# Encoder trunk on one core: the feed forward's activations turned by VectorE and memory in place of TensorE

## The chip, the core and the metric

The kernel runs on one core of a Trainium2 chip. The metric is device time in microseconds for one execution, median of three. TensorE (PE in the profile, PEld for its weight loads) multiplies, VectorE (DVE) and ScalarE (ACT) do the element work, SyncE (SP) issues the transfers between memory and the core, GpSimd (POOL) does little here.

## What is computed

Two layers over 256 tokens of 1024 features; the part that the change touches is the feed forward at the end of each layer:

```
def swiglu(hn, w_gu, w_down):
    g, u = jnp.split(hn @ w_gu, 2, axis=-1)
    return (jax.nn.silu(g) * u) @ w_down

for l in range(DEPTH):
    ...                                   # projections, three attentions, cross attention
    x = x + swiglu(rmsnorm(x, norm_ffn[l]), w_gu[l], w_down[l])
return rmsnorm(x, final_norm)
```

`w_gu` is 1024 x 5632, `w_down` is 2816 x 1024, all in float32.

## The kernel before

**Weights in chunks.** All weights lie in memory in the order of use, cut into 315 chunks of at most 128 x 1024 elements (512 KB). SP loads a chunk into one of 4 raw buffers (`wr`). ACT rounds it into `wh` (L192, fp32r) and DVE subtracts to get the rest, `wl` (L193); of these pairs there are 9. A product is three fast matmuls: `xh*wh`, `xh*wl`, `xl*wh` (L375, L376, L377). A chunk in the feed forward holds two blocks of 128 rows by 512 columns, so each half of the tokens needs six matmuls of it and both need twelve.

**Two halves.** The 256 tokens are two programs of 128 tokens, t = 0 and t = 1. They go through the chunks in the same order, t = 1 five calls behind (LAG); a chunk's buffer pair is free when t = 1 is through with it. `mm` yields before each chunk and calls `bg_step` after it; `defer(act)` puts an action off until the second such step after it.

**Feed forward.** For f = 0 to 4: four chunks of the gate weights give `ga`, then ACT takes the tanh (L795) and DVE multiplies (L796); four chunks of the up weights give `ua`, and DVE makes the activations `hh` (L805), 128 tokens x 512 features. f = 5 has 256 features and both parts in one product. The down projection needs `hh` with features on the partitions: `trans4` (L250) turns it by four TensorE transposes against the identity into PSUM (two for f = 5), and `split` rounds it into `hi` and `lo` (L241 on ACT, L242 on DVE). The six turned tiles of a half are the 22 blocks of features that the two products `fd0` and `fd1` then use.

**Order.** A scheduler sets the order of each engine's instructions at compile time, from priorities (program order, with `urgent` parts ahead) and its own estimate of when things are ready. Every engine, SP's queue of transfers included, works through its list in that order, and a waiting instruction holds up those behind it. `t2k` tiles (`t` in names) are 8 buffers that both halves share, `s2` tiles (`m`) are 11 for each half.

Of the kernel before, what the change touches and what calls it, by code (L numbers as in the profile page):

```python
# [12 lines left out]
F32 = mybir.dt.float32  # L13
F32R = mybir.dt.float32r
# [4 lines left out]
P = 128  # L19
# [18 lines left out]
LAG_OF = {(l, name): i + 1 for l in range(DEPTH) for i, name in enumerate(FIRST[l])}  # L38
WARM = 5
RAWBUFS = 4  # L40
AHEAD = 1
RAW_AHEAD = 4

# [68 lines left out]
def body(nc, tc, a, out, ctx):  # L112
# [4 lines left out]
    sb = ctx.enter_context(tc.tile_pool(name="sb", bufs=1))  # L117
    sm = ctx.enter_context(tc.tile_pool(name="sm", bufs=1))
    ps = ctx.enter_context(tc.tile_pool(name="ps", bufs=1, space=PS))
    V, S, T = nc.vector, nc.scalar, nc.tensor  # L120

    uid = [0]

    def nm(s):
        uid[0] += 1
        return f"{s}_{uid[0]}"

    def t2k(dtype=F32):
        return sb.tile([P, 512], dtype, name=nm("t"), tag="t2k", bufs=T2K)
# [4 lines left out]
    def psum(tag):  # L134
        return ps.tile([P, 512], F32, name=nm(tag), tag=tag, bufs={"acc": 3, "tp": 3, "sc": 2}[tag])
# [43 lines left out]
    def load_raw(c):  # L179
        g = c.group  # L180
        r = wp.tile([P, 1024], F32, name=nm("wr"), tag="wr", bufs=RAWBUFS)
        n = c.nkt * g.n
# [14 lines left out]
    def ensure(index):  # L197
        while split_next[0] <= min(index + AHEAD, len(chunks) - 1):
            i = split_next[0]
            while raw_next[0] <= min(i + RAW_AHEAD - 1, len(chunks) - 1):  # L200
                load_raw(chunks[raw_next[0]])
                raw_next[0] += 1
            split_chunk(i)
# [35 lines left out]
    def split(hi, lo, src, scale=None):  # L239
        if scale is None:  # L240
            S.activation(hi, src, AF.Copy)  # L241
            V.tensor_tensor(lo, src, hi.bitcast(F32), op=ALU.subtract)  # L242
        else:
            S.activation(hi, src, AF.Copy, scale=scale)
            V.scalar_tensor_tensor(lo, src, scale, hi.bitcast(F32), op0=ALU.mult, op1=ALU.subtract)

    def trans4(src, n=4, tag="tp"):
        tp = psum(tag)
        for i in range(n):
            T.transpose(tp[:, i * P:(i + 1) * P], src[:, i * P:(i + 1) * P], ident)  # L250
        return tp

    class Lhs:


# [7 lines left out]
    def split_tiles(t, tag, bufs):  # L263
        return (sb.tile([P, 512], F32R, name=nm("xh"), tag=f"{tag}{t}", bufs=bufs),
                sb.tile([P, 512], F32R, name=nm("xl"), tag=f"{tag}{t}", bufs=bufs))
# [50 lines left out]
    for p in range(4):  # L316
        hi, lo = split_tiles(p // 2, "x2_", X2BUFS)
# [17 lines left out]
    def program(t):  # L335
        bg = deque()

        later = deque()
# [8 lines left out]
                except StopIteration:  # L347
                    bg.popleft()

        def defer(act):  # L350

            later.append(lambda: later.append(act))

        def flush(gen):
            while later:
# [4 lines left out]
        def s2(dtype=F32):  # L360
            return sb.tile([P, 512], dtype, name=nm("m"), tag=f"m{t}", bufs=11)

        def mm(g, pairs):

            for c in g.chunks:
                yield
                ensure(c.index)
                hi, lo = splits[c.index]
                for lhs, acc in pairs:
                    for j in range(c.nkt):  # L370
                        kt = c.kt0 + j
                        xh, xl = lhs.blocks[kt]
                        wh, wl = hi[:, j * g.n:(j + 1) * g.n], lo[:, j * g.n:(j + 1) * g.n]
                        o = acc[:, :g.n]
                        T.matmul(o, xh, wh, start=kt == 0, stop=False)  # L375
                        T.matmul(o, xh, wl, start=False, stop=False)  # L376
                        T.matmul(o, xl, wh, start=False, stop=kt == g.kts - 1)  # L377
                bg_step()
# [51 lines left out]
        def pv_T(eTs, vs, pairs, nblk):  # L430

            in_line = line()
            o = psum("tp")
            with tc.high_priority(offset=150):
                for j, b in reversed(list(enumerate(pairs))):
                    for half in (1, 0):
                        c = (2 * b + half) * 64  # L440
                        for kb in reversed(range(nblk)):
                            in_line(T.matmul(o[half * 64:half * 64 + 64, j * P:(j + 1) * P], vs[kb][:, c:c + 64],  # L442
                                             eTs[half][j * nblk + kb], start=kb == nblk - 1, stop=kb == 0))
            return o
# [129 lines left out]
        for l in range(DEPTH):  # L574
# [34 lines left out]
            def indexer(acc):  # L609
                qi, ki = t2k(), t2k()  # L610
                rope(qi[:, :256], acc[:, :256], 4, rs8, t)
                rope(ki[:, :64], acc[:, 256:320], 1, rs, t)
                V.tensor_copy(ki[:, 64:128], ki[:, 0:64])
                V.tensor_scalar(wi[:, 0:4], acc[:, 320:324], rs[:, 0:1], 0.5, op0=ALU.mult, op1=ALU.mult)

                def turn_idx():
                    tp = psum("tp")
                    for i in range(2):
                        T.transpose(tp[:, i * P:(i + 1) * P], qi[:, i * P:(i + 1) * P], ident)
                    T.transpose(tp[:, 256:384], ki[:, 0:128], ident)  # L620
                    S.copy(qkiT, tp[:, 0:384])
                defer(turn_idx)

            branches = {}
            for br in "CBA":
# [3 lines left out]
                for name in FIRST[l] if br == "C" else [br + x for x in "qkv"]:  # L629
# [14 lines left out]
                    dst = s2()  # L644
                    if nme == "v":
                        S.activation(dst, acc, AF.Copy, scale=rs[:, 0:1])
                    else:
                        r_ = rs8 if nme == "q" else rs
                        tok = t2k()
                        if br == "A":  # L650
                            S.activation(tok, acc, AF.Copy, scale=r_[:, 0:1])
                        else:
                            rope(tok, acc, 8, r_, t)

                        def turn(tok=tok, dst=dst):
                            S.copy(dst, trans4(tok))
                        defer(turn)
# [7 lines left out]
                else:  # L665
                    gen = attn_A(l, ts_["q"])
                branches[br] = (gen, ts_["q"])
                defer(lambda gen=gen: bg.append(gen))

            y = None  # L670
# [24 lines left out]
            with urgent(t):  # L695
                for h in range(2):
                    tp = trans4(y[h])
                    hi, lo = split_tiles(t, "x2_", X2BUFS)
# [25 lines left out]
            if t == 0:  # L724
# [4 lines left out]
                for m in range(2):  # L729
                    tok = t2k()  # L730
                    S.activation(tok[:, :256], accs[m][:, :256], AF.Copy, scale=rsm[m])
                    tp = trans4(tok, 2)
# [6 lines left out]
            with urgent(t):  # L739
                qx, qxT = t2k(), t2k()  # L740
                S.activation(qx[:, :256], acc[:, :256], AF.Copy, scale=rs8[:, 0:1])
                tp = trans4(qx, 2)
# [28 lines left out]
            with urgent(t):  # L771
                eTs = [turn_over(e) for e in es]
                tp = pv_T(eTs, [vx[:, 0:256], vx[:, 256:512]], [0, 1], 2)
                hi, lo = split_tiles(t, "o2_", 2)
# [14 lines left out]
            for f in range(6):  # L789
                th, hh = t2k(), t2k()  # L790
                n = 512 if f < 5 else 256
                if f < 5:
                    ga = psum("acc")
                    yield from mm(G[f"fg{f}"], [(xf, ga)])
                    S.activation(th, ga, AF.Tanh, scale=rsh[:, 0:1])  # L795
                    V.scalar_tensor_tensor(th, th, 1.0, ga, op0=ALU.add, op1=ALU.mult)  # L796
                    ua = psum("acc")
                    yield from mm(G[f"fu{f}"], [(xf, ua)])
                else:
                    ga = psum("acc")  # L800
                    yield from mm(G["fgu"], [(xf, ga)])
                    S.activation(th[:, :n], ga[:, :n], AF.Tanh, scale=rsh[:, 0:1])
                    V.scalar_tensor_tensor(th[:, :n], th[:, :n], 1.0, ga[:, :n], op0=ALU.add, op1=ALU.mult)
                    ua = ga[:, n:2 * n]
                V.scalar_tensor_tensor(hh[:, :n], th[:, :n], rr2[:, 0:1], ua[:, :n], op0=ALU.mult, op1=ALU.mult)  # L805
                tp = trans4(hh, n // P)
                if f < 5:
                    hi, lo = s2(F32R), s2(F32R)
                else:
                    both = s2(F32R)  # L810
                    hi, lo = both[:, 0:256], both[:, 256:512]
                split(hi[:, :n], lo[:, :n], tp[:, :n])
                hT.add(hi, lo, n // P)
            ssq = small()
            xg = []
# [15 lines left out]
        for h, eng in enumerate((nc.scalar, nc.sync)):  # L831
            eng.dma_start(out[t * P:(t + 1) * P, h * 512:(h + 1) * 512], xg[h])

    progs = [program(0), program(1)]
    live = [True, True]

# [76 lines left out]
```

## Time and profile before

| | |
|---|---|
| median of 3 runs | 996.78 us (995.95 to 997.38) |
| profiled execution | 996.93 us, span 995.2 us |
| TensorE | busy 982.2 us (99%), granted clock 0.999 |
| VectorE, ScalarE | busy 661.1 us (66%), 561.2 us (56%) |
| transfers | 174.52 MB, mean 175 GB/s; SP's queue 55.4% of the 16 engines |
| feed forwards | first `hh` at 324.5 us, last at 937.6 us, in two stretches of some 115 us |

A row of the timeline gives the start, the time until the row's last instruction ends, engine, line and operation, the tiles written and read, the count, and in brackets the engine's idle time before and what ended it. Matmuls overlap: one that lasts 0.39 us is followed by the next after 0.23 us, so TensorE's pace is read from the starts.

### The profile page before, as it was taken

The numbers are of one execution on the slowest core, as the hardware profiler recorded it, in microseconds if no ns is written. First come the engines' busy times: TensorE is split into PE (matmuls) and PEld (weight loads), VectorE is DVE, ScalarE is ACT, GpSimd is POOL, SyncE is SP. The second block draws the span as 40 slices with busy tenths as digits, with TensorE's granted clock in tenths as the row PEclk, the third lists the DMA queues.
The fourth block names the chain that finished last, engine by engine and source line by source line (L and its number), as shares of the span: only waits on it lengthen the run. The fifth ranks groups of instructions, "written<-read, shape, count | busy, mean of one in ns | idle before, by whom it ended". The sixth has DMA issues, their size and how long they took to land.

```text
span 995.2 us, 13980 instructions
## 1 busy us (share of the span) xinstructions
PE 982.2 (99%) x5110; PEld 805.6 (81%) x5110; DVE 661.1 (66%) x1259; ACT 561.2 (56%) x985; POOL 14.0 (1%) x29
## 2 busy tenths in 40 slices
PE   8999999999999999999999999999999999999997
PEld 6887888888887888888888888888878778888885
DVE  5899666566866656554587995765676665656552
ACT  7546775555766544444554476764566764444441
POOL 0000000000000000000000000000000000000000
PEclk9999999999999999999999999999999999999999
DMA  8854445567662666666565545345566436656551
GB/s 301 281 185 149 142 133 150 151 189 236 207 188 71 205 177 188 188 178 191 174 209 200 168 131 166 128 150 168 190 214 191 147 106 191 190 175 208 188 169 43
DMA packets 50325, 174.52 MB, mean 175 GB/s; under 512 B 5712, under 2 KB 6608, under 8 KB 50000
## 3 DMA queue, kind: packets, MB, share of 16 engines
q1 hardware_dynamic: 49680, 172.94, 55.4%
q8 instruction: 40, 0.66, 0.3%
q10 hardware_dynamic: 576, 0.68, 0.2%
q14 instruction: 29, 0.24, 0.1%
HBM read 172.55 MB, written 1.05 MB: 174 GB/s over the span
## 4 chain that ended last, share of the span: by engine, by line
PE 90%; DVE 4%; DMA 2%; ACT 2%; issue 1%; SPq 0%; POOLq 0%; DVEq 0%; ACTq 0%
PE acc L375 27%; PE acc L376 27%; PE acc L377 26%; PE tp L250 4%; DVE wl L193 2%; PE tp L442 2%; PE sc L396 1%; DMA wr<-w_dram 1%; DMA t<-memT_dram 1%; PE sc L250 1%; PE tp L396 1%; ACT wh L192 1%; PE sc L748 1%; PE tp L426 1%; ACT m L276 0%
## 5 line engine op out<-in xcount | busy, mean ns | idle before, releaser
L193 DVE TENSOR_TENSOR wl<-wr,wh 128x1024 fp32r<-128x1024 f32 (+3 forms) x315 | 382.4, 1216 | 238.6 <-ACT wh L192 238.3
L192 ACT ACTIVATE wh<-wr 128x1024 fp32r<-128x1024 f32 (+3 forms) x315 | 331.6, 1054 | 262.2 <-PE acc L377 229.1
L375 PE MATMUL acc<-wh,xh 128*128 128x512 f32 (+2 forms) x1072 | 422.5, 395 | 1.7 <-ACT xh L276 0.9
L377 PE MATMUL acc<-wh,xl 128*128 128x512 f32 (+2 forms) x1072 | 416.3, 389 | 0.0
L376 PE MATMUL acc<-wl,xh 128*128 128x512 f32 (+2 forms) x1072 | 413.8, 387 | 2.0 <-DVE wl L193 2.0
L375 PEld LDWEIGHTS acc<-wh,xh 128*128 128x128 f32 x1072 | 202.0, 189 | 42.9 <-ACT xh L276 2.5
L376 PEld LDWEIGHTS acc<-wl,xh 128*128 128x128 f32 x1072 | 202.1, 189 | 41.6 <-DVE wl L193 4.2
L377 PEld LDWEIGHTS acc<-wh,xl 128*128 128x128 f32 x1072 | 201.6, 188 | 39.1 <-DVE xl L242 0.4
L375 PE MATMUL acc<-wh,m 128*128 128x512 f32 (+1 forms) x240 | 87.8, 366 | 0.0
L377 PE MATMUL acc<-wh,m 128*128 128x512 f32 (+1 forms) x240 | 87.6, 365 | 0.0
L376 PE MATMUL acc<-wl,m 128*128 128x512 f32 (+1 forms) x240 | 87.1, 363 | 0.0
L412 ACT ACTIVATE t<-t,s 128x128 f32<-128x128 f32 (+1 forms) x96 | 42.4, 444 | 19.5 <-DVE s L408 19.5
L375 PEld LDWEIGHTS acc<-wh,m 128*128 128x128 f32 x240 | 45.3, 189 | 7.8 <-issue 0.7
L376 PEld LDWEIGHTS acc<-wl,m 128*128 128x128 f32 x240 | 45.3, 189 | 7.0
L377 PEld LDWEIGHTS acc<-wh,m 128*128 128x128 f32 x240 | 45.3, 189 | 6.8
L250 PEld LDWEIGHTS tp<-ident,t 128*128 128x128 f32 x320 | 38.5, 141 | 13.6 <-DVE t L805 2.7
L250 PE MATMUL tp<-ident,t 128*128 128x128 f32 x320 | 49.5, 275 | 0.0
L276 ACT ACTIVATE xh<-sc,ctab 128x128 fp32r<-128x128 f32 x80 | 28.0, 360 | 17.4 <-DVE xl L277 12.7
L277 DVE SCALAR_TENSOR_TENSOR xl<-sc,ctab,xh 128x128 fp32r<-128x128 f32 x80 | 26.8, 346 | 6.3 <-ACT xh L276 5.6
L677 ACT ACTIVATE m<-acc,s 128x512 f32<-128x512 f32 x24 | 16.5, 688 | 19.5 <-PE acc L377 19.5
L563 DVE TENSOR_TENSOR x<-x,acc 128x512 f32<-128x512 f32 x24 | 16.4, 683 | 15.0 <-PE acc L377 14.8
L287 ACT ACTIVATE t<-x 128x512 f32<-128x512 f32 x28 | 17.4, 622 | 14.1 <-DVE x L563 13.9
(127 smaller groups left out, 630.5 us busy)
## 6 DMA issues: line engine op xcount, KB each, us to landing
wr<-w_dram SPq DMA_DIRECT2D x307, 512.0 KB, 3.7
bias<-bias_dram SPq DMA_DIRECT2D x2, 1024.0 KB, 7.3
t<-memT_dram SPq DMA_DIRECT2D x8, 256.0 KB, 5.1
wr<-w_dram SPq DMA_DIRECT2D x4, 486.0 KB, 5.1
x<-x_dram SPq DMA_DIRECT2D x4, 256.0 KB, 6.6
t<-mem_dram SPq DMA_DIRECT2D x4, 256.0 KB, 4.4
t<-xT_dram SPq DMA_DIRECT2D x3, 256.0 KB, 5.8
wr<-w_dram SPq DMA_DIRECT2D x2, 324.0 KB, 4.2
```

Source lines behind the costliest of these rows:

```text
L192: S.activation(hi[:, :n], r[:, :n], AF.Copy)
L193: V.tensor_tensor(lo[:, :n], r[:, :n], hi[:, :n].bitcast(F32), op=ALU.subtract)
L250: T.transpose(tp[:, i * P:(i + 1) * P], src[:, i * P:(i + 1) * P], ident)
L276: S.activation(hi[:, seg], src[:, seg], AF.Copy, scale=g)
L277: V.scalar_tensor_tensor(lo[:, seg], src[:, seg], g, hi[:, seg].bitcast(F32), op0=ALU.mult, op1=ALU.subtract)
L287: S.activation(junk, src, AF.Square, scale=1.0 / 32.0, accum_out=ssq[:, h:h + 1])
L375: T.matmul(o, xh, wh, start=kt == 0, stop=False)
L376: T.matmul(o, xh, wl, start=False, stop=False)
L377: T.matmul(o, xl, wh, start=False, stop=kt == g.kts - 1)
L396: T.matmul(sc[:, j * nk + kb * P:j * nk + (kb + 1) * P], qT[o:o + 64, b * P:(b + 1) * P], kTs[kb](o, b), start=True, stop=True)
L412: S.activation(e[:, seg], e[:, seg], AF.Exp, scale=-1.0, bias=nmax[:, j:j + 1], accum_out=ssum[:, j:j + 1])
L442: in_line(T.matmul(o[half * 64:half * 64 + 64, j * P:(j + 1) * P], vs[kb][:, c:c + 64], eTs[half][j * nblk + kb], start=kb == nblk - 1, st ...
```

## The change

`hh` is no longer turned by TensorE. VectorE transposes the sixteen 32 x 32 blocks of `hh` in one instruction and writes them to `th`, whose values are used up. SP writes `th` to a buffer in memory (256 KB), and four loads of 32 partitions each (64 KB, pieces of 512 bytes; half of that for f = 5) bring the blocks back into `hh` in the order that gives the full transpose. `split` then reads `hh` instead of PSUM, its output in an order of blocks, and it is put off until the fifth step after (`TURN`). All five transfers go through SP's queue.

```
+TURN = 4
...
+    dr = ctx.enter_context(tc.tile_pool(name="dr", bufs=1, space=bass.MemoryType.DRAM))
...
+    def turn_blocks(src, tmp, n=4):
+        V.transpose(tmp[:, :n * P].rearrange("p (j f s) -> p f j s", j=4, f=n),
+                    src[:, :n * P].rearrange("p (f j r) -> p f j r", f=n, j=4))
+        via = dr.tile([P, 512], F32, name=nm("via"), tag="via", bufs=8)
+        nc.sync.dma_start(via[:, :n * P], tmp[:, :n * P])
+        for j in range(4):
+            nc.sync.dma_start(src[j * 32:j * 32 + 32, :n * P].rearrange("r (i c) -> r i c", i=4),
+                              via[:, j * n * 32:(j + 1) * n * 32].rearrange("(i r) c -> r i c", i=4))
+        return src[:, :n * P].rearrange("p (i f s) -> p i f s", i=4, f=n)
+
+    def by_block(dst):
+        return dst.rearrange("p (f i s) -> p i f s", i=4, s=32)
...
-        def defer(act):
-            later.append(lambda: later.append(act))
+        def defer(act, n=1):
+            later.append((lambda: defer(act, n - 1)) if n else act)
...
-                tp = trans4(hh, n // P)
+                turned = turn_blocks(hh, th, n // P)
...
-                split(hi[:, :n], lo[:, :n], tp[:, :n])
+                defer(lambda hi=hi, lo=lo, turned=turned: split(by_block(hi), by_block(lo), turned), TURN)
```

Outside the feed forwards the order of the instructions on every engine stays as it was. Inside, three places matter. Line numbers after the change are higher: L185 is the load of a chunk, L194 and L195 its rounding, L296 and L297 the norm's (before: L183, L192, L193, L276, L277), L825 makes `hh`, L260 is the block transpose, L263 the write, L265 the loads, L243 and L244 the rounding of `hi` and `lo`.

SP's queue in the middle of the first feed forward, before:

```order
L183 DMA wr_841_3708<-w_dram 128x1024
L183 DMA wr_844_3726<-w_dram 128x1024
L183 DMA wr_853_3757<-w_dram 128x1024
L183 DMA wr_856_3775<-w_dram 128x1024
L183 DMA wr_860_3796<-w_dram 128x1024
L183 DMA wr_863_3814<-w_dram 128x1024
```

and now (`t_800` is `th` and `t_801` is `hh` of t = 1, `t_812` and `t_813` those of t = 0, one f further):

```order
L185 DMA wr_841_3716<-w_dram 128x1024
L185 DMA wr_844_3734<-w_dram 128x1024
L263 DMA via_835_3705<-t_800_3533 128x512
L185 DMA wr_853_3765<-w_dram 128x1024
L265 DMA t_801_3534<-via_835_3705 32x4x128 x4
L263 DMA via_847_3748<-t_812_3576 128x512
L185 DMA wr_856_3783<-w_dram 128x1024
L185 DMA wr_860_3804<-w_dram 128x1024
L265 DMA t_813_3577<-via_847_3748 32x4x128 x4
L185 DMA wr_863_3824<-w_dram 128x1024
```

Ten transfers of `hh` now stand among four loads of weights, and the loads of later chunks behind them.

ScalarE's list at the same place (`m_836` is `hi` of t = 1), before:

```order
L192 ACTIVATE wh_845_3728<-wr_829_3659 128x1024
L241 ACTIVATE m_836_3701<-tp_835_3696 128x512
L192 ACTIVATE wh_854_3759<-wr_832_3677 128x1024
L192 ACTIVATE wh_857_3777<-wr_841_3708 128x1024
```

and now:

```order
L194 ACTIVATE wh_854_3767<-wr_832_3685 128x1024
L194 ACTIVATE wh_857_3785<-wr_841_3716 128x1024
L194 ACTIVATE wh_861_3806<-wr_844_3734 128x1024
L243 ACTIVATE m_836_3711<-t_801_3534 128x4x4x32
L815 ACTIVATE t_838_3713<-acc_840_3715,s_760_3351 128x512
L194 ACTIVATE wh_864_3826<-wr_853_3765 128x1024
```

The rounding of `hh` (`m_836`) has moved behind the rounding of three more chunks; the tanh of the next f and the rounding of chunk `wr_853` stand behind it.

VectorE's list at the start of the first feed forward, where t = 0 makes its first `hh` (`t_707`) while t = 1 still has its norm (`xl_751`, `xl_754`), before:

```order
L805 SCALAR_TENSOR_TENSOR t_707_3134<-t_706_3133,s_705_3131,acc_735_3244 128x512
L277 SCALAR_TENSOR_TENSOR xl_751_3316<-sc_749_3310,ctab_74,xh_750_3315 128x128
L277 SCALAR_TENSOR_TENSOR xl_754_3331<-sc_752_3325,ctab_74,xh_753_3330 128x128
L297 TENSOR_SCALAR s_760_3349<-s_759_3346 128x1
L193 TENSOR_TENSOR wl_779_3408<-wr_746_3291,wh_778_3407 128x1024
```

and now:

```order
L825 SCALAR_TENSOR_TENSOR t_707_3136<-t_706_3135,s_705_3133,acc_735_3246 128x512
L297 SCALAR_TENSOR_TENSOR xl_751_3318<-sc_749_3312,ctab_76,xh_750_3317 128x128
L297 SCALAR_TENSOR_TENSOR xl_754_3333<-sc_752_3327,ctab_76,xh_753_3332 128x128
L317 TENSOR_SCALAR s_760_3351<-s_759_3348 128x1
L260 STREAM_TRANSPOSE t_706_3135<-t_707_3136 128x4x4x32
L297 SCALAR_TENSOR_TENSOR xl_751_3318<-sc_749_3312,ctab_76,xh_750_3317 128x128
L297 SCALAR_TENSOR_TENSOR xl_754_3333<-sc_752_3327,ctab_76,xh_753_3332 128x128
L807 TENSOR_TENSOR s_761_3353<-s_759_3348,s_760_3351 128x1
L195 TENSOR_TENSOR wl_779_3410<-wr_746_3293,wh_778_3409 128x1024
```

The block transpose and the next pieces of the norm now stand ahead of the subtraction for chunk `wr_746`.

## Rows read from the trace of the kernel before

**Rows 1.** Page, parts 1 and 4: busy time by engine; chain that ended last

```profile
PE 982.2 (99%) x5110; PEld 805.6 (81%) x5110; DVE 661.1 (66%) x1259; ACT 561.2 (56%) x985; POOL 14.0 (1%) x29
...
PE 90%; DVE 4%; DMA 2%; ACT 2%; issue 1%; SPq 0%; POOLq 0%; DVEq 0%; ACTq 0%
```

**Rows 2.** Busy time by engine in a stretch of each feed forward; clock, DMA share, GB/s

```profile
330.00:430.00 100.00, 100.00 (x456) 81.86 (x456) 60.49 (x64) 48.48 (x55) 0.00 (x0) 1.00 0.62 185
820.00:920.00 100.00, 100.00 (x455) 81.79 (x454) 60.95 (x63) 48.35 (x54) 0.00 (x0) 1.00 0.60 192
```

**Rows 3.** Timeline of TensorE around three groups of transposes

```profile
343.43 0.39 PE L375 MATMUL acc<-wh,xh 128*128 128x512 f32 x1
343.66 0.39 PE L376 MATMUL acc<-wl,xh 128*128 128x512 f32 x1
343.89 0.60 PE L250 MATMUL tp<-ident,t 128*128 128x128 f32 x4
344.25 0.48 PE L377 MATMUL acc<-wh,xl 128*128 128x512 f32 x1
344.56 0.40 PE L375 MATMUL acc<-wh,xh 128*128 128x512 f32 x1
...
371.77 0.39 PE L376 MATMUL acc<-wl,xh 128*128 128x512 f32 x1
372.06 0.66 PE L250 MATMUL tp<-ident,t 128*128 128x128 f32 x4
372.47 0.48 PE L377 MATMUL acc<-wh,xl 128*128 128x512 f32 x1
372.79 0.40 PE L375 MATMUL acc<-wh,xh 128*128 128x512 f32 x1
...
938.00 0.39 PE L376 MATMUL acc<-wl,m 128*128 128x512 f32 x1
938.23 0.38 PE L250 MATMUL tp<-ident,t 128*128 128x128 f32 x2
938.37 0.48 PE L377 MATMUL acc<-wh,m 128*128 128x512 f32 x1
938.68 0.39 PE L375 MATMUL acc<-wh,m 128*128 128x512 f32 x1
```

**Rows 4.** Waits, the row of the transposes: waited for, us in total, times, longest

```profile
PEld tp L250 <- DVE t L805: 2.7, 9, 0.4
```

**Rows 5.** Lines of VectorE and ScalarE, 330 to 430 us: count, busy us, mean ns, idle

```profile
L193 DVE TENSOR_TENSOR wl<-wr,wh 128x1024 fp32r<-128x1024 f32 x37 | 45.3, 1226 | 33.1 <-ACT wh L192 33.1
L805 DVE SCALAR_TENSOR_TENSOR t<-t,s,acc 128x512 f32<-128x512 f32 x8 | 5.9, 744 | 1.6 <-PE acc L377 1.6
L242 DVE TENSOR_TENSOR m<-tp,m 128x512 fp32r<-128x512 f32 x8 | 5.5, 683 | 0.0
L192 ACT ACTIVATE wh<-wr 128x1024 fp32r<-128x1024 f32 x36 | 38.1, 1060 | 40.3 <-PE acc L377 40.3
L795 ACT ACTIVATE t<-acc,s 128x512 f32<-128x512 f32 x9 | 6.2, 690 | 9.3 <-PE acc L377 9.3
L241 ACT ACTIVATE m<-tp 128x512 fp32r<-128x512 f32 x8 | 4.8, 600 | 2.0 <-PE tp L250 2.0
```

**Rows 6.** Timeline at the first feed forward's start, VectorE's and TensorE's rows

```profile
325.66 0.14 DVE L297 TENSOR_SCALAR s<-s 128x1 f32<-128x1 f32 x1
...
326.02 1.23 DVE L193 TENSOR_TENSOR wl<-wr,wh 128x1024 fp32r<-128x1024 f32 x1 [0.22 <-ACT wh L192]
327.16 0.60 DVE L277 SCALAR_TENSOR_TENSOR xl<-sc,ctab,xh 128x128 fp32r<-128x128 f32 x2
...
327.68 0.15 DVE L787 TENSOR_TENSOR s<-s,s 128x1 f32<-128x1 f32 x1
...
328.24 0.40 PE L376 MATMUL acc<-wl,xh 128*128 128x512 f32 x1
```

**Rows 7.** Waits of SP's queue

```profile
SPq L183 <- DVE wl L193: 565.5, 225, 12.1
```

**Rows 8.** Tile wr from 330 to 430 us: issues on SP, time to landing

```profile
L183 SPq DMA_DIRECT2D wr<-w_dram x36: 327/328/328, 330.6 to 428.5; - x36
...
DMA to landing us min/median/max: 3.5/3.9/4.7
```

**Rows 9.** Page, part 6, transfers: engine, count, KB each, median us to landing

```profile
bias<-bias_dram SPq DMA_DIRECT2D x2, 1024.0 KB, 7.3
...
out_dram<-t SPq DMA_DIRECT2D x2, 256.0 KB, 2.1
...
subln<-subln_dram SPq DMA_DIRECT2D x2, 64.0 KB, 4.4
```

More of the change, by code (lines that the diff above doesn't have):

```diff
@@ L805, in program @@
                 V.scalar_tensor_tensor(hh[:, :n], th[:, :n], rr2[:, 0:1], ua[:, :n], op0=ALU.mult, op1=ALU.mult)
-                tp = trans4(hh, n // P)
+                turned = turn_blocks(hh, th, n // P)
                 if f < 5:
-                    hi, lo = s2(F32R), s2(F32R)
+                    hi, lo = s2(F32R)[:, :], s2(F32R)[:, :]
                 else:
```

## The prediction

> **What bounds the kernel now.** I read the page first: TensorE is busy for 99% of the span, and the chain that ended last lies on TensorE for 90% [rows 1]. Then the busy time in a stretch of each feed forward: TensorE 100%, at a granted clock of 1.00 (the 2.4 GHz level), VectorE 60%, ScalarE 48%, transfers 62% [rows 2]. So in the stage that changes, time is what TensorE's list of instructions takes, and an engine beside it matters only where it makes TensorE wait. The timeline of TensorE says what one instruction is worth there: matmuls start every 0.23 us [rows 3], and a chunk of twelve takes about 2.72 us (37 chunks in 100 us, [rows 5]).
>
> **What goes.** 20 groups of four transposes and 4 of two leave TensorE's list. A group's price is read from the starts around it, less the two usual steps of 0.23 us. Without a wait: 343.66 to 344.56 is 0.90, less 0.46, so 0.44 to 0.45 us. Where it waits for VectorE: 371.77 to 372.79 is 1.02, so 0.56 us. With two transposes: 938.00 to 938.68 is 0.68, so 0.22 us [rows 3]. Waits of this kind are counted nine times [rows 4], for one half's groups of nearly every f, so I take half of them with it: 10 x 0.45 + 10 x 0.56 + 4 x 0.22 = 11.0 us go. All of it was on the path, since TensorE had no idle time in these stretches.
>
> **The block transposes.** VectorE gets 24. The trace has none. The nearest row by size and type is the subtraction L242 with 0.68 us for 512 columns [rows 5]; if the sixteen blocks went one by one at the 0.14 us of VectorE's smallest row [rows 6] it would be 2.2 us, and if two elements went at a time 0.34 us. I take 0.68. Per f (21.8 us) VectorE would have 8 x 1.23 for weights and 2 x 2.8 for both halves (L796, L805, L242 at about 0.7 each [rows 5], and the block transpose), 71%: no bound. In the steady part a late subtraction has cover: 9 buffer pairs, t = 1 six chunks behind (its first of the five calls only brings it to its first chunk), so a pair comes free two chunks, 5.4 us, before t = 0 needs it again, and rounding takes 1.06 + 1.23 us [rows 5]. Some 3 us are spare, more than any of the values above.
>
> Not so at the start of each feed forward. There the subtraction for a chunk began at 326.02 and TensorE used its result at 328.24 [rows 6]. By the new order the block transpose, the two pieces of the norm and the small product come first. VectorE was done with the row before at 325.80: plus 0.68, 0.60, 0.15 and 1.23 is 328.46. TensorE, without the transposes just before, would be there at 328.24 - 0.54, about 327.7. So it waits about 0.75 us, twice in the kernel: 1.5 us lost (0.8 if the transpose takes 0.34, 4.6 if 2.2).
>
> **The rounding of `hh`.** L241 and L242 (0.60 and 0.68 us) read the core's own memory instead of PSUM, in pieces of 32; no row shows that, and I cost the difference at nothing, since both engines are idle over a third of the stage [rows 2]. What covers them if they take twice as long is the same 3 us.
>
> **The detour through memory** is the real question, because engines work in order. Count from the end of the up product of t = 1. L805 takes 0.74 us and the block transpose 0.68; VectorE can be inside a subtraction then (up to 1.2). The write starts at 1.6 to 2.8, I take 2.2. It lands 2.1 us later by the write of the output with the same size [rows 9], up to 3.9 by a chunk of weights of twice the size amid traffic [rows 8]; I take 3.0, nearer the like-sized row. The four loads need 4 x 0.4 us to issue (0.33 each, [rows 8], and a little between). The last lands 2.1 to 7.3 us after issue; the row that is like it is subln, 64 KB in 128 pieces of 512 bytes, 4.4 us [rows 9]. Together 2.2 + 3.0 + 1.6 + 4.4 = 11.2 us (bounds 7.4 and 15.6).
>
> When is it too late? ScalarE's new list has the rounding of `hh` behind six later chunks, then the tanh, then the seventh chunk's rounding. TensorE starts that chunk six chunks later, at about 16.2 us, and needs `wl` with its second matmul at 16.4. Before it lie 0.60 (L241), 0.69 (tanh), 1.06 and 1.23 [rows 5]: the blocks must have landed by 12.8 us. 11.2 leaves 1.6. ScalarE would reach the rounding at about 9 us and idle for two, which costs TensorE nothing.
>
> **SP's queue.** SP waits in place: its 565.5 us of waiting before weight loads are waits for a free raw buffer, with all later loads behind them [rows 7]. Now a write waits for VectorE and the first load for the write, with the weights behind. The Trainium skill, "DMA: Bandwidth & Descriptors", section "Anatomy of one DMA — SWDGE (gpsimd) path", says the same as a rule against this change: DMA engines never wait on a semaphore, the wait is spent on the issuing sequencer. The trace agrees, with the 565.5 us. What does it cost? The chunk behind the second write goes out at about 2.2 + 3.0 + 1.6 + 0.8 = 7.6 us; it lands by 12.3 at the slowest 4.7 [rows 8], and its rounding must start by 19.1 - 2.3 = 16.8. The load behind the second group of loads goes out at about 12.5 and has until 22 us. Now a load goes out four chunks (10.9 us) ahead of its own subtraction and needs 3.9 + 2.3 of that. So SP's queue costs nothing as long as a write lands in 7 us. The extra bytes (12 MB on 174.5) raise the transfers' share from 62% [rows 2] to perhaps 75%.
>
> **Sum.** 996.93 (span 995.2 and what lies around it) - 11.0 + 1.5 = 987.4 us for the profiled execution. It was 0.15 above the median of the runs, so I predict 987.2 us. The steps alone bound it at 986.6 and 990.3 (block transpose); a few tenths either way for what TensorE's other waits do.
>
> **Rivals.**
> (a) The blocks land late and ScalarE stands still. Place: L243 for t = 1, with a chunk's rounding behind it, five times in each layer. Price: each us after 12.8 is a us of TensorE, ten times. It decides from 1.0 us too late, which takes back the whole 9.6. For it: small pieces, weights of 512 KB ahead in the same queue, and the 7.3 us of the 1 MB row [rows 9]. With 7.3 the blocks land at 14.1, 1.3 late, 13 us lost: 1000 us, slower. Against it: the like-sized row has 4.4, and the stretch has bandwidth to spare. 8%.
> (b) The four loads go one after another, each with its full time: 4 x 2.1 by the shortest row [rows 9] is 8.4 instead of 6.0 us, landing at 13.6, 0.8 late, 8 us lost: 995.4 us, no change. Against it: SP issues every 0.4 us without waiting for a landing. The Trainium skill, same page, section "Rules for kernel authors", asks to coalesce transfers under 64 KB because they are mostly overhead; its fixed 2.0 us for each would give nearly the same time. No row here shows four small loads in a row. 6%.
> (c) Weights late behind SP's waits: a write that took 8.3 us to land would hold the next chunk a us past its time, ten times: 997 us. No row of that size takes so long. 2%.
> (d) Half the gain goes to new waits for VectorE in the steady part, because the block transpose takes 2.5 us or more and its neighbours meet it: 992 us. 8%.
>
> **Chances.** Forecast 76%, its own range 985.5 to 990.3. About 0.2% (2 us) is what a measurement of this kernel can tell from no change, so faster means below 994.8: forecast, (d) and a part of (b) together 86%; within 6%; slower 8%. The range for 8 in 10: 985 to 993.
>
> **What would show it.** Right: TensorE's instructions fall from 5110 to 5022, its busy time by about 10 us; no wait of TensorE for VectorE's transposes; at the start of each feed forward one wait of 0.5 to 1 us for `wl`; a block transpose of about 0.7 us; write landing in 2 to 4 us, loads in 3 to 5; ScalarE waits for a load of `via` a little, and TensorE's starts stay 0.23 us apart. Wrong: idle time of TensorE before L395 to L397 in each f, ended by `wl` or `wh`, behind a ScalarE wait for a transfer. (a) shows as ScalarE's L243 waiting over 3 us, (b) as loads landing about 2 us apart, (c) as L194 waiting for `wr`, (d) as VectorE's L260 of over 2 us.

## The result, and the profile after

The changed kernel takes 984.9 us (median, 984.2 to 985.7) against 996.8 before: a ratio of 0.9877, 95% interval 0.9865 to 0.9889. That is 11.9 us less, where 9.6 were forecast; the time lies 2.3 us under the forecast. The profiled execution took 984.2 us, its span 982.4.

The page of the changed kernel answers to [rows 1]; its last two rows are the new transfers (line, engine, operation, count, KB each, median us from issue to landing):

```profile
PE 970.0 (99%) x5022; PEld 796.7 (81%) x5022; DVE 675.0 (69%) x1283; ACT 559.9 (57%) x985; POOL 14.0 (1%) x29
...
PE 90%; DVE 4%; DMA 2%; ACT 2%; issue 1%; SPq 0%; POOLq 0%; DVEq 0%; ACTq 0%
...
via<-t SPq DMA_DIRECT2D x20, 256.0 KB, 2.7
t<-via SPq DMA_DIRECT2D x80, 64.0 KB, 4.3
```

TensorE lost the 88 transposes and 12.2 us of busy time, and it still carries 90% of the chain. The same two stretches as in [rows 2]:

```profile
330.00:430.00 100.00, 100.00 (x442) 82.79 (x442) 69.31 (x76) 49.95 (x56) 0.00 (x0) 1.00 0.81 243
820.00:920.00 100.00, 100.00 (x443) 82.81 (x442) 68.97 (x77) 48.90 (x55) 0.00 (x0) 1.00 0.78 246
```

TensorE stays at 100% and at a granted clock of 1.00. VectorE went from 60% to 69% and the transfers from 62% to 81% (75% was forecast); neither makes TensorE wait. To see where the time went I laid the n-th weight matmul of the changed kernel beside the n-th of the kernel before (3936 in each) and read by how much its start had moved: 0.7 us earlier ahead of the first feed forward (the first loads of the execution), 5.9 us within the first feed forward, 0.2 between the two, 6.0 within the second. Each group of four took 0.46 to 0.50 us with it for t = 1; for t = 0 it took 0.57 to 0.63, except the first of each feed forward, 0.45 and 0.47; a group of two took 0.39, or 0.25 and 0.27. These add up to the 11.9 us, so the whole gain is the transposes' own time.

The detour itself, first on SP's queue for one f (start, time until the row's last instruction ends, engine, line, operation, tiles, count):

```profile
343.34 0.33 SPq L263 DMA_DIRECT2D via<-t  x1
344.44 0.33 SPq L185 DMA_DIRECT2D wr<-w_dram  x1
347.85 1.75 SPq L265 DMA_DIRECT2D t<-via  x4
349.69 0.38 SPq L263 DMA_DIRECT2D via<-t  x1
350.17 0.87 SPq L185 DMA_DIRECT2D wr<-w_dram  x2
351.96 1.75 SPq L265 DMA_DIRECT2D t<-via  x4
```

then VectorE,

```profile
341.82 0.75 DVE L825 SCALAR_TENSOR_TENSOR t<-t,s,acc 128x512 f32<-128x512 f32 x1 [0.35 <-PE acc L397]
342.60 0.71 DVE L260 STREAM_TRANSPOSE t<-t 128x512 f32<-128x512 f32 x1
343.23 1.18 DVE L195 TENSOR_TENSOR wl<-wr,wh 128x1024 fp32r<-128x1024 f32 x1
```

and ScalarE:

```profile
349.97 1.06 ACT L194 ACTIVATE wh<-wr 128x1024 fp32r<-128x1024 f32 x1 [1.61 <-PE acc L397]
351.34 0.63 ACT L243 ACTIVATE m<-t 128x512 fp32r<-128x512 f32 x1 [0.30 <-DMA t<-via]
352.69 0.69 ACT L815 ACTIVATE t<-acc,s 128x512 f32<-128x512 f32 x1 [0.72 <-PE acc L397]
```

From the start of L825 to ScalarE's rounding are 9.5 us, and ScalarE waited 0.30 us for the last load, as one row says; over the whole kernel it waits 0.5 us in two places for these loads. The write goes out at 343.34 and the first load, behind a chunk of weights, at 347.85, when the write has landed. The block transpose takes 0.71 us.

### The profile page after: what moved, and what is told of

Same layout as the page of the kernel before. It is cut to its first block, busy times and chain, and to the rows that moved or that the text cites. A ratio compares the mean times of both kernels' runs of the same rounds, so it can differ in the third digit from the quotient of the medians.

```text
span 982.4 us, 14062 instructions
## 1 busy us (share of the span) xinstructions
PE 970.0 (99%) x5022; PEld 796.7 (81%) x5022; DVE 675.0 (69%) x1283; ACT 559.9 (57%) x985; POOL 14.0 (1%) x29
## 4 chain that ended last, share of the span: by engine, by line
PE 90%; DVE 4%; DMA 2%; ACT 2%; issue 1%; SPq 0%; POOLq 0%; DVEq 0%; ACTq 0%
PE acc L395 27%; PE acc L396 27%; PE acc L397 27%; PE tp L252 3%; DVE wl L195 2%; PE tp L462 2%; PE sc L416 1%; DMA wr<-w_dram 1%; DMA t<-memT_dram 1%; PE sc L252 1%; PE tp L416 1%; PE sc L768 1%; ACT wh L194 1%; PE tp L446 1%; ACT m L296 0%
## 5 line engine op out<-in xcount | busy, mean ns | idle before, releaser
L195 DVE TENSOR_TENSOR wl<-wr,wh 128x1024 fp32r<-128x1024 f32 (+3 forms) x315 | 382.0, 1214 | 218.6 <-ACT wh L194 215.5
L194 ACT ACTIVATE wh<-wr 128x1024 fp32r<-128x1024 f32 (+3 forms) x315 | 331.6, 1054 | 264.2 <-PE acc L397 214.2
L296 ACT ACTIVATE xh<-sc,ctab 128x128 fp32r<-128x128 f32 x80 | 28.0, 361 | 16.7 <-DVE xl L297 11.9
L252 PE MATMUL tp<-ident,t 128*128 128x128 f32 x232 | 35.6, 274 | 0.0
L252 PEld LDWEIGHTS tp<-ident,t 128*128 128x128 f32 x232 | 28.2, 140 | 8.8 <-ACT t L761 1.2
L297 DVE SCALAR_TENSOR_TENSOR xl<-sc,ctab,xh 128x128 fp32r<-128x128 f32 x80 | 26.8, 345 | 6.2 <-ACT xh L296 5.6
```

What stands on the lines that cost most here:

```text
L194: S.activation(hi[:, :n], r[:, :n], AF.Copy)
L195: V.tensor_tensor(lo[:, :n], r[:, :n], hi[:, :n].bitcast(F32), op=ALU.subtract)
L296: S.activation(hi[:, seg], src[:, seg], AF.Copy, scale=g)
L297: V.scalar_tensor_tensor(lo[:, seg], src[:, seg], g, hi[:, seg].bitcast(F32), op0=ALU.mult, op1=ALU.subtract)
```

## The experiments

**1. The transposes put back.** TensorE turns `hh` again beside the detour, into PSUM that nobody reads; all that the change added stays.

```
+                trans4(hh, n // P)
                 turned = turn_blocks(hh, th, n // P)
```

> The changed kernel with the 88 TensorE transposes put back beside the new way; nothing reads what they write. Theory (hidden detour): of all that was added nothing lies on TensorE's path, and the gain of 11.9 us is the transposes' own time alone. Then putting them back restores the time before: 996.8 us, between 996.0 and 997.6. Rival (a loss at the starts, as the prediction had it): the removal was worth 13.4 us, of which 1.5 were lost to the block transposes at the two starts; then this kernel has both, 984.9 + 13.4 = 998.3 us.

Measured: 996.98 us, ratio to the kernel before 1.000 (0.9991 to 1.0009). The gain is what the transposes cost TensorE, to within 0.9 us by this interval.

**2. No turning at all.** The rounding reads `hh` as it is, without block transpose, write and loads (and so not the turned values).

```
-                turned = turn_blocks(hh, th, n // P)
+                turned = hh[:, :n].rearrange("p (i f s) -> p i f s", i=4, f=n // P)
```

> Leaves the transposition of the activations out altogether: no TensorE transposes, no block transposes, no transfers; the rounding reads the activations as they are, put off as in the changed kernel. Theory (hidden detour): the added parts cost nothing, so leaving them out gives nothing: 984.9 us, within 0.8. Rival (a loss at the starts): 1.5 us come back, 983.4 us.

Measured: 985.16 us (0.9878, 0.9865 to 0.9892). Without anything that was added the kernel is no faster: block transposes, 120 more transfers and the waits on SP's queue cost nothing that a difference of about 1 us would show.

**3. One and three extra block transposes at the start.** For f = 0 of t = 0 in each feed forward, where the prediction saw a wait of 0.75 us.

```
+        for _ in range(times):      # times: 2 or 4 for (f, t) == (0, 0), else 1
             V.transpose(...)
```

> One block transpose more for t = 0, f = 0 in each layer, at the place in VectorE's list where the prediction saw a loss; with it one piece of the norm (0.35 us) also moves ahead of the subtraction for the chunk behind. Theory (hidden detour): in the changed kernel that subtraction ended 0.81 us before the first matmul that reads it; 0.71 + 0.35 use that up and make TensorE wait 0.25 us, twice: 985.4 us. Rival (a loss at the starts): TensorE already waits there, so all of 1.06 us is added, twice: 987.0 us. The wait itself is in the trace: 0.2 to 0.3 us against 1.1 or more.

> Three block transposes more at the same place; by the order two of them and the piece of the norm (1.77 us) come ahead of the subtraction, one behind it. Theory (hidden detour): 1.77 - 0.81 = about 0.96 us of waiting at each start, 1.9 us in all: 986.8 us. Rival (a loss at the starts): all of 1.77, twice: 988.4 us. In the trace one wait of TensorE of 0.9 to 1.0 us at each start, against 1.8 or more.

Measured: 984.83 (0.9864 to 0.9891) and 985.07 us (0.9865 to 0.9896). Both readings missed. The order of TensorE's instructions tells why: the group that reads the delayed subtraction stood in row 1463 of TensorE's list in the changed kernel, four rows later with one extra and in row 1469 with three. The scheduler, by its own estimate, put other matmuls ahead of it, so the delay didn't meet the group that it was meant for. With three extra the subtraction ended at 329.03 and was first used at 329.76.

**4. The same with TensorE's order held.** Three extra block transposes as before; in addition three groups of matmuls in that stretch (the last chunk of `fg0` and the first of `fu0` for t = 1, the third of `fg1` for t = 0) are tied behind the matmul that the text puts ahead of them. TensorE's whole list is then the changed kernel's.

```
+    if j == 0 and placed and ((t == 1 and c in (G["fg0"].chunks[-1], G["fu0"].chunks[0]))
+                              or (t == 0 and c is G["fg1"].chunks[2])):
+        tc.add_manual_dep(first.ins, placed[-1].ins.name, NoSync, ...)
```

> Three extra block transposes in the first chunk of each feed forward, as before, and three pairs of matmul groups there tied to their order in the text, so that TensorE's instruction order is now the changed kernel's own (with the three extra alone the scheduler had moved the group that reads the subtraction six rows back). The subtraction should end at about 329.0, as it did with three extra, and TensorE wants it at 328.24, where 0.81 us was to spare. Theory (the delay at the start is real, but 2.14 us of slack stood before it, not 0.75 us less than none): TensorE waits about 0.8 us at each of two starts, 986.5 us. Rival (TensorE's wait there is swallowed later in the feed forward): 984.9 us. The prediction's own reading (no slack at all): 2 x 2.1 more, 989 us.

Measured: 986.28 us (985.8 to 987.9; 0.9881 to 0.9910), 1.4 over the changed kernel (1.1 if each is set against the kernel before in its own series). That is little beside the spread of the times; the trace shows it better. TensorE's timeline at the place:

```profile
328.57 0.39 PE L404 MATMUL acc<-wh,xl 128*128 128x512 f32 x1
329.48 0.50 PE L403 MATMUL acc<-wl,xh 128*128 128x512 f32 x1 [0.53 <-DVE wl L195]
329.82 0.40 PE L404 MATMUL acc<-wh,xl 128*128 128x512 f32 x1
```

and VectorE's:

```profile
327.63 0.70 DVE L263 STREAM_TRANSPOSE t<-t 128x512 f32<-128x512 f32 x1
328.25 1.18 DVE L195 TENSOR_TENSOR wl<-wr,wh 128x1024 fp32r<-128x1024 f32 x1
```

The subtraction ends at 329.43 and TensorE starts at 329.48, 0.91 after the matmul before it, where 0.23 is the pace. Laid beside the changed kernel, the matmuls move back by 0.78 us here and by 0.80 at the second start, 1.6 us together, and never catch up. So the mechanism that the prediction gave for the starts exists; it needs some 1.6 us more of delay than the prediction thought (0.75 late in the prediction, 0.81 to spare in the changed kernel).

**5. The rounding without deferral.** `TURN = 0` for 4: written at the first step behind the loads in place of the fifth.

> The rounding is written down in the same chunk as the subtraction instead of four calls of the list later; the scheduler gives the same instruction order on every engine in the steady state, since it places the rounding by its own estimate of when the four loads land. Theory (the deferral in the text of the program does nothing, the scheduler sets the place): 984.9 us, as with five chunks. Rival (the number of chunks in the text matters, the rounding comes too early and ScalarE waits): several us more, 990 to 1000.

Measured: 984.38 us (0.9858 to 0.9891). The order of the instructions in the steady state is the same. The five steps in the text do nothing here; the scheduler puts the rounding where it expects the loads.

**6. The rounding tied to an early place.** Every later chunk's weight rounding on ScalarE has to stand behind the last rounding of `hh`, which is deferred with 2 in place of 4 ("two calls") or with 1 ("one").

```
-        S.activation(hi[:, :n], r[:, :n], AF.Copy)
+        ins = S.activation(hi[:, :n], r[:, :n], AF.Copy)
+        if rounded: behind(ins, rounded[-1])
-                defer(..., 4)
+                defer(round_now, 2)      # or 1; round_now appends to rounded
```

> The rounding is deferred by two calls and tied down: every later chunk's weight rounding on ScalarE has to stand behind it, so ScalarE's list can't be filled with chunks ahead of it. By the trace of the changed kernel the loads of the t=1 half land 9.7 us after its up product and those of t=0 16.8 us; ScalarE would have to go on by 8.0 and 13.4 us for the weights behind it to be ready. Theory (a late block stalls ScalarE and through the weights TensorE; the rival of the prediction with ScalarE's stalls): 1.7 to 5.1 us for each of ten pairs, 17 to 51 us more, 1002 to 1036 us. Rival (the weights' buffers and the 27 us until the transposed block is needed swallow it): 984.9 us.

> The rounding tied one chunk earlier than in the kernel that ties it with two, so the block is wanted 2.7 us sooner at each of ten pairs. There ScalarE waited 39.5 us in 13 places for the loads and the time rose by 6.0 us: the weights that ScalarE had prepared ahead swallowed five sixths. Theory (the slack is spent once, further delay goes straight to TensorE): 10 x 2.7 = 27 us on top, about 1018 us. Rival (the same share is swallowed): 6.0 + 27 x 0.15 = 10 us over the changed kernel, about 995 us.

Measured: 990.93 us (0.9932 to 0.9962) with two, 996.88 (0.9987 to 1.0010) with one. What ScalarE's rounding waited for, with two calls:

```profile
  DMA t<-via: 39.5, 13
  DVE t L269: 1.5, 1
  DVE wl L204: 1.3, 1
  DVE t L832: 0.5, 1
```

TensorE's waits in the same kernel (engine, tile and line waited for; us in total, times, longest):

```profile
PE acc L404 <- ACT wh L201: 2.6, 7, 0.7
PE acc L405 <- DVE wl L204: 2.4, 6, 0.5
```

and for one call the waits of the weight loads into TensorE:

```profile
PEld acc L405 <- DVE wl L204: 17.5, 32, 1.0
PEld tp L261 <- issue: 5.2, 16, 0.8
PEld acc L404 <- ACT wh L201: 4.4, 4, 1.5
```

ScalarE stands still for a late block, and TensorE then waits for weights: this is the mechanism of the prediction's rival (a). By the starts, neighbouring weight matmuls in the two feed forwards stand 0.7 us in all over their pace of 0.23 in the changed kernel, 7.0 with two calls and 14.3 with one, so the loss lies there. Its size is less than a us for a us: 39.5 us of ScalarE's waiting cost 6.0 us, where the expectation had 17 or more by its own limit for the blocks, and one call earlier cost 6 more, where it had 27. For two calls both expectations were wrong (17 to 51 us, or none), for one call the rival's 995 us came nearer than the theory's 1018. The tie also changes the order of other work on ScalarE, VectorE and TensorE, so the share that is swallowed is a measurement of these two kernels, not a law.

**7. A longer detour.** One more copy of 256 KB in memory ahead of the loads.

```
+        first = dr.tile([P, 512], F32, ...)
+        nc.sync.dma_start(first[:, :n * P], tmp[:, :n * P])
-        nc.sync.dma_start(via[:, :n * P], tmp[:, :n * P])
+        nc.sync.dma_start(via[:, :n * P], first[:, :n * P])
```

> One more copy of 256 KB in memory stands between the subtraction and the four loads on SP's queue, so the detour is 3 to 5 us longer and SP's queue is held that much longer at each of 20 groups. Theory (the weights stand at least 4 us ahead and the rounding is placed by the scheduler's estimate, which grows with the copy): 984.9 us, within 1 us. Rival (SP's queue is in order, the weights behind the held loads come late; the third rival of the prediction): 20 groups by 0.5 us or more, 995 us or slower.

Measured: 984.64 us (0.9866 to 0.9895). The copy takes 3.5 us, and ScalarE's waits for weights from memory grew:

```profile
ACT wh L194 <- DMA wr<-w_dram: 30.7, 35, 2.7
```

In the changed kernel that row is 13.4 us in 15 places. Seventeen us more of ScalarE's waiting, and nothing at the end that these runs can tell (about 1 us): SP's queue is no bound even with the copy.

**8. The same way for q and k.** The token tiles of q and k in the attentions, 22 groups of four, are turned in blocks too (all but one of the first layer).

```
-                            def turn(tok=tok, dst=dst):
-                                S.copy(dst, trans4(tok))
-                            defer(turn)
+                            turned = turn_blocks(tok, dst)
+                            defer(lambda dst=dst, turned=turned: S.copy(by_block(dst[:, :]), turned), TURN)
```

> The same way is taken for the token tiles of q and k in the attentions, all but one of the first layer: 22 more groups of four transposes leave TensorE. Theory (a group is worth 0.45 to 0.57 us of TensorE's time wherever the detour is hidden): 22 x 0.47 = 10.4 us less, 974.6 us. Rival (the attentions use what is turned within a few us, so TensorE or ScalarE waits for the loads): no gain or slower, 985 to 1000 us.

Measured: 979.04 us (978.4 to 980.9; 0.9811 to 0.9841), 1.7% under the kernel before and the fastest here. It is 5.9 us under the changed kernel for 22 groups, 0.27 us each, not 0.47. ScalarE's waits:

```profile
ACT wh L194 <- DMA wr<-w_dram: 29.2, 26, 3.3
...
ACT m L681 <- DMA t<-via: 6.0, 3, 4.0
```

and TensorE's (1.7 and 1.5 us, where the changed kernel has 1.4 and 0.5):

```profile
PE acc L396 <- DVE wl L195: 1.7, 4, 0.5
PE acc L395 <- ACT wh L194: 1.5, 3, 0.7
```

These waits explain 1.3 of the 4.5 us that are missing. Counted from the starts, the time by which small matmuls hold two neighbouring weight matmuls apart fell by only 5.4 us: the runs of plain transposes lost 7.3 us for 88 instructions (0.33 us for four, since some of them stood in longer runs), and the scores, cut into 19 runs for 14, took 2 more.

**9. Branches A and B alone.**

```
-                        if (l, name) == (0, "Ck"):
+                        if br == "C":
```

> Only the q and k tiles of two of the three branches (A and B) are turned by the new way, 16 groups beside the 20 of the feed forward; branch C keeps TensorE's transposes. With all three, 22 groups gave 5.9 us, 0.27 us each; score matmuls were cut into more pieces (19 interruptions of the long matmuls for 14) and ScalarE waited 6.0 us for loads. Theory (branch C causes those losses): 16 x 0.45 = 7.2 us, 977.7 us, faster than with all three. Rival (every group in an attention is worth only 0.27 us): 980.6 us.

Measured: 981.70 us (981.0 to 983.9; 0.9835 to 0.9866), 3.2 us for 16 groups, 0.20 each. Branch C isn't what costs. ScalarE waits 7.6 us for loads here, with the scores in 14 runs as before, and the rival's price for a group came nearer. By the starts the 16 groups took 5.1 us with them, 0.32 each as in experiment 8; but TensorE's two waits for `wl` and `wh` that stood at 1.4 and 0.5 us in the changed kernel are 2.6 and 1.2 here.

**10. q and k through GpSimd's queue.**

```
-                            turned = turn_blocks(tok, dst)
+                            turned = turn_blocks(tok, dst, q=nc.gpsimd)
```

> The q and k tiles of all branches by the new way as before, but their write and four loads are issued on GpSimd's queue instead of SP's, on which ScalarE's waits for weights had grown from 13.4 to 29.2 us. Theory (weights held behind the loads on SP's queue cost about 1.5 us of TensorE's idle time): 977.5 us. Rival (the loss is in how small matmuls are cut, and SP's queue costs nothing, as in the feed forward): 979.0 us; if GpSimd's issue is slow the blocks come later and it is slower.

Measured: 1013.27 us (1012.3 to 1017.3; 1.0147 to 1.0194), slower than before. The transfers of that queue land about as soon as SP's in the same run (2.8 and 3.9 us for the same sizes), by the page:

```profile
via<-m POOLq DMA_DIRECT2D x22, 256.0 KB, 3.3
t<-via POOLq DMA_DIRECT2D x88, 64.0 KB, 4.0
```

but GpSimd's timeline shows how late they start:

```profile
62.95 0.56 POOL L263 DMA_DIRECT2D via<-m  x1 [0.97 <-DVE work L527]
67.81 2.18 POOL L265 DMA_DIRECT2D t<-via  x4 [4.30 <-DMA via<-m]
77.28 0.56 POOL L263 DMA_DIRECT2D via<-m  x1 [7.29 <-DVE m L260]
```

An issue costs GpSimd 0.55 us (SP 0.42), each group's loads stand in one list behind the waits of the others, and ScalarE waits:

```profile
ACT m L681 <- DMA t<-via: 49.2, 16, 9.4
```

TensorE then waits 12.7 us for `wl`, in ten places. Around the end of four of its idle stretches, of 2.3 to 3.4 us, its granted clock also fell to 0.50, the 1.2 GHz level, for 3.4 us each; no other kernel's profile here has that before its very end. An estimate from these rows: 13.6 us at half speed cost 6.8 us at most. Moving the detour off SP's queue made it worse; which part of the 34 us is GpSimd's issue and which its waits isn't told apart.

## Why the prediction was right and wrong

**The transposes' time (forecast -11.0).** Right in kind, 0.9 us too small: 11.9 by the matmuls' starts, and putting the transposes back gives all of it back. About 0.4 of the 0.9 lies in the four groups of two (0.25 to 0.39 where 0.22 was read from the one shown) and about as much in those of t = 1 (0.46 to 0.50 where [rows 3] gave 0.45). The ten of t = 0 came to 5.7 us, where 5.6 was forecast: eight were worth about 0.60 each, the first of each feed forward 0.46.

**The wait at the start of each feed forward (forecast +1.5).** This is the step that failed, and with the 0.9 us it makes the 2.3 us of the miss: measured, the wait is 0. The step said that "TensorE used its result at 328.24" [rows 6]. It didn't. The two halves' matmuls alternate there, and L376 at 328.24 read another chunk, of the half that lags. TensorE's list before the change, from row 1456 (tile names with their numbers; 3355 is t = 1, 3398 is t = 0, and 3408 the chunk in question):

```
1456 L375 MATMUL acc_3398<-wh_3407,xh_3095
1457 L377 MATMUL acc_3355<-wh_3139,xl_3316
1458 L375 MATMUL acc_3355<-wh_3163,xh_3330
1459 L376 MATMUL acc_3355<-wl_3164,xh_3330
...
1463 L377 MATMUL acc_3355<-wh_3163,xl_3331
1464 L376 MATMUL acc_3398<-wl_3408,xh_3095
```

and the trace of the same matmuls:

```profile
327.55 0.39 PE L375 MATMUL acc<-wh,xh 128*128 128x512 f32 x1
327.77 0.40 PE L377 MATMUL acc<-wh,xl 128*128 128x512 f32 x1
328.01 0.39 PE L375 MATMUL acc<-wh,xh 128*128 128x512 f32 x1
328.24 0.40 PE L376 MATMUL acc<-wl,xh 128*128 128x512 f32 x1
...
329.38 0.39 PE L376 MATMUL acc<-wl,xh 128*128 128x512 f32 x1
```

The pattern of lines says which is which: the first use is row 1464, the L376 at 329.38. The subtraction had ended at 327.25 (326.02 and 1.23), 2.1 us ahead. After the change it ended at 327.43 and TensorE got there at 328.24, the group ahead of it gone (and 0.7 us of lead from the first loads): 0.81 us are left. The step let the change take 1.75 us from this place, from 1.0 to spare (328.24 less 327.25) to 0.75 late. The change took 1.3, and there were 2.1 to take; even the step's own 1.75 would have left 0.4. VectorE's row after the change, and TensorE's first use:

```profile
326.21 1.22 DVE L195 TENSOR_TENSOR wl<-wr,wh 128x1024 fp32r<-128x1024 f32 x1
...
328.24 0.39 PE L396 MATMUL acc<-wl,xh 128*128 128x512 f32 x1
```

Three more transposes with TensorE's order held used the 0.8 up and cost 1.6 us by the starts (1.4 by the times), the 1.6 that this slack says.

**The block transpose and the rounding.** 0.68 us for the block transpose by the nearest row, 0.71 measured; for 256 columns 0.44. The rounding in pieces of 32, whose difference the prediction put at nothing, took 0.61 us on ScalarE (L243) and 0.68 on VectorE (L244), against 0.60 and 0.68 before.

**The detour.** The last block landed 9.4 us after the start of L825 in the f shown (8.1 to 11.9 over all groups), where 11.2 after the product was forecast and 12.8 was the limit; ScalarE idled 0.3 us, where two were forecast. The write took 2.6 us (1.7 to 4.4) for 3.0, the loads 0.42 us to issue and 4.5 (1.9 to 6.2) to land for 4.4. The four loads overlap, which settles rival (b): in every group they landed 0.2 to 0.9 us apart, where the rival had about 2. Rival (a) didn't come; its mechanism shows when the order is forced (experiment 6), at less than a us for a us of waiting. The limit of 12.8 belongs to the changed kernel's order, in which no block was late, so the price behind it wasn't tested. Rival (c) didn't come, not even with a longer detour (experiment 7); rival (d) needed a block transpose of 2.5 us. The rule of the Trainium skill on waits in the issuing sequencer ("DMA: Bandwidth & Descriptors", "Anatomy of one DMA — SWDGE (gpsimd) path") agrees with the trace after, where SP's queue itself waits for block transposes and for writes:

```profile
SPq L263 <- DVE t L260: 29.7, 15, 4.8
SPq L265 <- DMA via<-t: 27.1, 22, 3.0
```

It cost nothing there. The rule on small transfers in the same page of the Trainium skill ("Rules for kernel authors") asks to coalesce them, since under 64 KB one pays mostly overhead. Read as one fixed cost after another it gave rival (b). The trace doesn't bear that reading out: four were issued within 1.75 us, and all had landed 3.4 and 6.3 us after the first issue in the two groups shown. The 2.0 us that the prediction took from that page is its figure for transfers that GpSimd issues; these went out on SP's queue.

**What wasn't forecast.** That the deferral in the text decides nothing (experiment 5).

## What to carry to other kernels

Where one engine is busy all the time, count what leaves its list, from the starts of its own instructions; what was put on engines with slack cost nothing here, since every result still came before its first use. That first use must be found by the tile and its number, not by the next row of the right line: where two halves alternate, neighbouring rows of one line belong to different work. And a gain read in one stage isn't the gain in another: four transposes were worth 0.45 to 0.63 us inside a steady stream of large matmuls, and taking them out of the attentions left 0.20 to 0.27.

## What the runs showed that was not expected

- Little of ScalarE's waiting reaches the end: 39.5 us in 13 places cost 6.0, and 17 us more of waits for weights cost nothing that the runs can tell. That the nine pairs of buffers, with rounded weights ahead, swallow the rest is argued and not shown.
- The scheduler moves TensorE's matmuls around a delay that it foresees. One or three extra VectorE instructions cost nothing; with TensorE's order held, three cost 1.4 us.
- Four loads of 64 KB from one buffer, 0.42 us apart at issue, land 0.2 to 0.9 us apart.
- 22 detours through GpSimd's queue cost 34 us against the same detours through SP's, with about the same time to land; in four places the granted clock of TensorE fell with them.
